# A hybrid convolution and mLSTM block: gate loads by another queue, end loads within the output projection, turns one step later, left sums in the plain stage

## The chip, the cores and the metric

The kernel runs on one core of a Trainium2 chip. The metric is device time in microseconds (us) of one execution. The engines are TensorE (PE, matrix multiplication; PEld is its weight load), VectorE (DVE), ScalarE (ACT), GpSimd (POOL) and SyncE (SP, which here only issues DMAs). Each engine works through its own queue in order. GpSimd and ACT can issue DMAs too.

## The reference

All tensors are float32; 512 tokens of 1024 features, one layer.

```python
hn = rmsnorm(x, g_mix)
proj = hn @ w_in                     # 14344 columns
(xa, ba, ca, za, q, k, v, o, zb, ig, fg, ga, gb) = split(proj)
ya = (ba * causal_short_conv(ca * xa) * silu(za)) @ w_a_out
hb = rmsnorm(mlstm_chunkwise(q, k, v, ig, fg))          # 4 heads
yb = (sigmoid(o) * hb * silu(zb)) @ w_b_out             # 2048 -> 1024
merged = sigmoid(ga) * ya + sigmoid(gb) * yb
x = x + merged @ w_o
gate = sigmoid(rmsnorm(x, g_ple) @ w_ple_gate)
x = x + gate * (p @ w_ple)
return rmsnorm(x, g_final)
```

## The kernel before

**Stages.** The work runs in one order on PE: the start and the projections of the mLSTM (0 to 100 us), its heads (to 455), the projection of ga (to 480), four convolution stages (to 642), the plain stage `w_a_out` (to 690), the heads' output `w_b_out` (to 772), the output projection `w_o` (to 815), the gate of the embedding (to 858), and the end.

**Matmuls.** Each float32 product is made of three (`mm3`, L205 to L207): both operands are cut into a high and a low part. The high part of the weights is made by ACT (`whi`, L152), the low part by DVE (`wlo`, L153), from a raw piece `wraw` that SP loads (L135) into one of four buffers. Most big products are Strassen's: seven products in place of eight, of which some need a sum of two weight pieces. The second piece is then added by an accumulating DMA that GpSimd issues (L159), or by DVE (L157). `out` makes a combined output `c` (L325) on DVE from a snapshot that ACT takes of a PSUM bank (L321: `s`, `v`).

**Order.** The engines' order is the order in which the program is written. PE works in blocks (in `w_b_out` and `w_o`, twelve matmuls of 512 columns), and after each block `step()` calls `tick()`: it starts the tasks that the block before it set off, then cuts one half of a weight piece, then takes one `yield` further each generator in `active`. So one more `yield` puts what follows one block later on every engine.

**Convolution** (`sink_conv`). `third` keeps a product `cg` in a temporary with the tag `v`, the tag of the snapshots of L321; `fourth` keeps `cx` with the tag `e`. L382 (`put`) reads `cg` last. `m`, the merged tensor of four 128x1024 rows of tokens, is in place by then and is first written in the plain stage.

**Gates.** `sink_gate(g)` writes the sigmoids of ga and gb to DRAM (`sg_d`, L716), issued by GpSimd: `sink_gate(0)` for gb early, `sink_gate(2)` for ga right before the convolution. The plain stage loads those of ga (`sga`, L985, SP) and writes m (L988). In `w_b_out`, `sink_heads` multiplies a gate of gb with the output (L1023) and adds it to m (L1024). Its gates `sgb` have two buffers, and SP loads each (L1005) after the one before it in the same buffer is used.

**Turn.** Once two rows of m are complete, `turn_half` transposes them on PE (`pth`, L1014) and cuts the result into `mg`, the left operand of `w_o`.

**Left sums.** Strassen's left operands of `w_b_out` come from `yf`, four 128x2048 tiles, and `hsf` (shown as `yhs`). `left_first` makes the first three and four differences in the plain stage, `left_heads` the others in `w_b_out` (`left_high` on ACT, `low` on DVE at L951), and four sums on DVE (L976, L980).

**Loads for the end.** Right after `w_b_out`'s code GpSimd's queue has x (`xr`, four rows of 512 KB, L1057), `gfin` (L1059) and the embedding `ple` (2 MB in one, L1061).

Of the kernel before, what the change touches and what calls it, by code (L numbers as in the profile page):

```python
# [36 lines left out]
def hybrid_block(ctx, tc, x, p, g_mix, w_in, conv_w, conv_b, w_a_out, b_gates, g_head,  # L37
# [17 lines left out]
    def close(*cs):  # L55
        for c in cs:
            c.__exit__(None, None, None)
# [200 lines left out]
    def temp(tag, name=None, dt=F32):  # L258

        return tp.tile([P, S], dt, name=name or tag, tag=tag, bufs={"c": 3}.get(tag, 2))  # L260
# [19 lines left out]
    def block_tm(lhs, post):  # L280

        pss = [None] * NT
        for c, (parts, k0) in enumerate(lhs):
            w = next_operand()
            for t in range(NT):
                if c == 0:
                    pss[t] = bank(t)
                for kt in range(HC):
                    mm3(pss[t], [u[:, k0 + kt, t * P:(t + 1) * P] for u in parts], [u[kt] for u in w],
                        c == 0 and kt == 0, c == len(lhs) - 1 and kt == HC - 1)  # L290
                step(post(t, pss[t]) if c == len(lhs) - 1 else None)
# [68 lines left out]
        product(6, acc, None, lambda i: sink(0, 2 + i, acc[i]))  # L360
        order.reverse()

    def sink_conv(c, u, v, ya):


        w = [[cw[:, j * KT + c + f:j * KT + c + f + 1] for j in range(3)] for f in range(2)]
        b = [cb[:, c + f:c + f + 1] for f in range(2)]
        part = [slice(f * H2, (f + 1) * H2) for f in range(2)]
        held = {}

        def taps(f):
            to = v[:, part[f]]
            dve.tensor_scalar(to, u[:, f, 2:], w[f][2], None, ALU.mult)
            for j in range(2):
                dve.scalar_tensor_tensor(to, u[:, f, j:j + H2], w[f][j], to, ALU.mult, ALU.add)

        def put(src, h):
            to = [t[:, c:c + 2, h * H2:(h + 1) * H2] for t in ya]
            src = src.rearrange("p (f s) -> p f s", f=2)
            act.activation(to[0], src, AF.Copy)  # L380
            yield
            dve.tensor_tensor(to[1], src, to[0].bitcast(F32), ALU.subtract)  # L382

        def split(t):
            return t.rearrange("p (f s) -> p f s", f=2)

        def first(i, src):
            if i == 0:
                held["x"] = src
                return  # L390
            dve.memset(u[:, :, :2], 0.0)
            dve.tensor_tensor(u[:, :, 2:], split(held["x"]), split(src), ALU.mult)
            for f in range(2):
                yield
                taps(f)

        def second(i, src):
            if i == 0:
                for f in range(2):
                    dve.scalar_tensor_tensor(v[:, part[f]], v[:, part[f]], b[f], src[:, part[f]], ALU.add, ALU.mult)  # L400
                return
            z = temp("e", "cz")
            act.activation(z, src, AF.Sigmoid)
            dve.tensor_tensor(v, v, src, ALU.mult)
            yield
            dve.tensor_tensor(v, v, z, ALU.mult)
            yield
            yield from put(v, 0)

        def third(i, src):  # L410
            if i == 0:
                held["b"] = src
                return
            z = temp("e", "cz")
            act.activation(z, src, AF.Sigmoid)
            g = held["g"] = temp("v", "cg")
            dve.tensor_tensor(g, held["b"], src, ALU.mult)
            yield
            dve.tensor_tensor(g, g, z, ALU.mult)

        def fourth(i, src):
            if i == 0:
                held["x"] = temp("e", "cx")
                act.activation(held["x"], src, AF.Copy)
                yield
                return
            dve.tensor_copy(u[:, :, :2], u[:, :, H2:])
            dve.tensor_tensor(u[:, :, 2:], split(held["x"]), split(src), ALU.mult)
            g = held["g"]
            for f in range(2):  # L430
                yield
                taps(f)
            yield
            for f in range(2):
                dve.scalar_tensor_tensor(g[:, part[f]], v[:, part[f]], b[f], g[:, part[f]], ALU.add, ALU.mult)
            yield
            yield from put(g, 1)

        def sink(n, t, src):
            yield from ((first, fourth), (second, third))[n][t // 2](t % 2, src)  # L440
        return sink
# [270 lines left out]
    def sink_gate(g):  # L712
        def sink(n, t, src):
            sg = temp("e", "sg") if n == 0 and t > 1 else src
            act.activation(sg, src, AF.Sigmoid)
            nc.gpsimd.dma_start(sg_d[g + n][:, t, :], sg)  # L716
            yield
        return sink

# [207 lines left out]
    cv_ctx, cvp = open_pool("conv")  # L927
    cu = cvp.tile([P, 2, H2 + 2], F32, name="cu")
    cv = cvp.tile([P, S], F32, name="cv")
    for c in range(0, KT, 2):  # L930
        strassen(hn_lhs, sink_conv(c, cu, cv, ya), True)
    close(hs_ctx, hn_ctx)


# [7 lines left out]
    def left_high(k):  # L942

        j, g = divmod(k, 2)
        a11, a21, a12, a22 = (yf[2 * g + r][:, v] for r, v in ((0, 0), (0, 1), (1, 0), (1, 1)))
        src = (a11, a12, hsf[g], a12, hsf[g], a21, a22)[j]
        both = wbp.tile([P, 2, HC, H2], F32R, name=f"l{k}", tag=f"ring{k % 3}", align_bytes=256)
        units[k] = [both[:, u] for u in range(2)]
        scale = -1.0 if j == 4 else 1.0
        act.activation(units[k][0], src, AF.Copy, scale=scale)  # L950
        return lambda: dve.scalar_tensor_tensor(both[:, 1], src, scale, both[:, 0].bitcast(F32), ALU.mult, ALU.subtract)  # L951

    def left_first():
        for _ in range(5):
            yield
        for k in range(3):
            low = left_high(k)
            yield
            low()
            yield  # L960
        for g in range(2):
            (a11, a21), a22 = (yf[2 * g][:, v] for v in range(2)), yf[2 * g + 1][:, 1]
            dve.tensor_tensor(hsf[g], a22, a21, ALU.subtract)
            yield
            dve.tensor_tensor(a21, a11, a21, ALU.subtract)
            yield

    def left_heads():
        yield
        yield  # L970
        for k in range(3, 14):
            low = left_high(k)
            yield
            low()
            if k in (4, 5):
                dve.tensor_tensor(hsf[k - 4], hsf[k - 4], yf[2 * (k - 4)][:, 0], ALU.add)  # L976
            yield
            if k in (4, 5):
                a12 = yf[2 * (k - 4) + 1][:, 0]
                dve.tensor_tensor(a12, hsf[k - 4], a12, ALU.subtract)  # L980

    def gate_conv(n):
        sga = [temp(u, "sga") for u in "sscc"]
# [6 lines left out]
        return post  # L990

    active.append(left_first())
    for n in range(2):
        block_tm([(ya, 0), (ya, HC)], gate_conv(n))


    mg = [hp.tile([P, KT, S], F32R, name=f"mg{i}", tag=t, align_bytes=256) for i, t in enumerate(("qk", "vv"))]
    sgb = deque()
    todo = deque((n, t) for n, ts in ((0, (0, 1)), (1, range(NT)), (0, (2, 3))) for t in ts)

    def load_gate():
        if todo:
            n, t = todo.popleft()
            sgb.append(temp("e", "sgb"))
            nc.sync.dma_start(sgb[-1], sg_d[n][:, t, :])  # L1005

    def turn_half(dst, src, n, h):

        ss = slice(h * H2, (h + 1) * H2)
# [10 lines left out]
    def sink_heads(n, t, src):  # L1020
        sg = sgb.popleft()
        mc = m[:, t, n * CW:(n + 1) * CW]
        dve.tensor_tensor(sg, sg, src, ALU.mult)  # L1023
        dve.tensor_tensor(mc, mc, sg, ALU.add)  # L1024
        load_gate()
        yield
        if t % 2:
            yield from turn_half(mg, m, n, t // 2)

    for _ in range(2):  # L1030
        load_gate()
    active.append(left_heads())
    strassen(units, sink_heads, groups=2)
    close(wb_ctx, cv_ctx)

    def turn_to(dst, src, n, scale):

# [15 lines left out]
    h2_ctx, h2p = open_pool("h2", side="right")  # L1053
    h2 = [h2p.tile([P, KT, S], F32R, name=f"h2_{i}", align_bytes=256) for i in range(2)]
    xr = ep.tile([P, NT, D], F32, name="xr")
    for t in range(NT):
        nc.gpsimd.dma_start(xr[:, t, :], x[0, t * P:(t + 1) * P, :])  # L1057
    gfin = ep.tile([P, D], F32, name="gfin")
    nc.gpsimd.dma_start(gfin, g_final.partition_broadcast(P))  # L1059
    ple = ep.tile([P, NT, D], F32, name="ple")  # L1060
    nc.gpsimd.dma_start(ple, ple_d)  # L1061
    ess = ep.tile([P, NT, 2], F32, name="ess")
    etot = ep.tile([P, NT], F32, name="etot")
    er = ep.tile([P, NT], F32, name="er")
    etmp = [ep.tile([P, NT], F32, name=f"etmp{i}") for i in range(3)]
    half = [slice(0, CW), slice(CW, D)]

    def add_residual(n):
        def post(t, ps):
# [6 lines left out]

    post = add_residual(0)
    pss = [None] * NT  # L1080
    w = {}
# [147 lines left out]
```

## Time and profile before

| what | value |
|---|---|
| runs | 882.72, 883.28, 887.46 us; median 883.28 |
| profiled execution | 882.37 us, span 880.6 us |
| mean granted clock of PE | 0.993 of full speed |
| PE, DVE, ACT, POOL busy | 97%, 68%, 53%, 29% of the span |
| bytes moved by DMA | 169.65 MB, 193 GB/s on the mean |

A busy share is a mean over all stages; where PE has no work is found by its waits. In a row of a timeline stand start and duration, engine, line and operation, what is written and read, the shapes, and in brackets the idle time ahead of it with what ended it. In an answer of the chain stand start, duration and the step.

### The profile page before, as it was taken

The page shows a single profiled execution, that of the slowest core. Times are in us where ns is not written, and L with a number is a line of the kernel's source. Part 1 is how long each engine was busy: PE and PEld are TensorE (multiplying, and loading weights), DVE is VectorE, ACT ScalarE, POOL GpSimd, SP SyncE. Part 2 cuts the span into 40 slices and gives each one's busy share as a digit, 9 for nine tenths or more (in the row PEclk, how much of TensorE's full clock was granted, in tenths as well). Part 3 has the DMA queues.
Part 4 walks back from the last instruction along what each step waited for, and adds up shares of the span by engine and source line. Part 5 has one row for each costly group of instructions (what it writes and reads, how often), then busy time and mean ns, then how long its engine had stood idle before and what let it go on. Part 6 is the DMA issues. An engine that isn't in the chain of part 4 may idle for free.

```text
span 880.6 us, 11798 instructions
## 1 busy us (share of the span) xinstructions
PE 853.2 (97%) x4507; PEld 731.8 (83%) x4507; DVE 600.2 (68%) x774; ACT 467.9 (53%) x674; POOL 253.2 (29%) x239
## 2 busy tenths in 40 slices
PE   7999999999999999999999999999999999879995
PEld 6877888888888888888888999999988878668885
DVE  5769586765673757836875678888876597744465
ACT  6475774646636565556665464545542555514342
POOL 4641423232322314223333424334201124100031
PEclk9999999999999999999999999999999999989998
DMA  9798987968747778787879989898995689962002
GB/s 294 257 223 222 288 207 155 217 211 189 201 144 176 150 176 188 226 192 169 205 176 249 223 176 175 200 173 183 208 379 158 124 207 197 369 224 96 1 1 96
DMA packets 100232, 169.65 MB, mean 193 GB/s; under 512 B 6160, under 2 KB 44112, under 8 KB 98768
## 3 DMA queue, kind: packets, MB, share of 16 engines
q0 software_dynamic: 38816, 76.03, 44.5%
q1 hardware_dynamic: 61360, 92.87, 31.8%
q8 instruction: 35, 0.57, 0.3%
q14 instruction: 21, 0.17, 0.1%
HBM read 153.16 MB, written 15.73 MB: 192 GB/s over the span
## 4 chain that ended last, share of the span: by engine, by line
PE 76%; DVE 9%; DMA 6%; issue 5%; ACT 3%; POOL 1%; POOLq 0%; SPq 0%; DVEq 0%; ACTq 0%
PE mm L207 23%; PE mm L206 23%; PE mm L205 23%; DVE wlo L153 4%; DMA wraw<-in_w_b_out 2%; ACT whi L152 2%; DMA wraw<-in_w_in 2%; DMA sgb<-sg_d 1%; PE pv L205 1%; PE pv L206 1%; PE pv L207 1%; PE pty L744 1%; POOL wraw L159 1%; DVE l L951 1%; PE sc L207 1%
## 5 line engine op out<-in xcount | busy, mean ns | idle before, releaser
L153 DVE TENSOR_TENSOR wlo<-wraw,whi 128x1024 fp32r<-128x1024 f32 x234 | 299.1, 1282 | 133.3 <-ACT whi L152 133.1
L152 ACT ACTIVATE whi<-wraw 128x1024 fp32r<-128x1024 f32 x236 | 246.3, 1053 | 94.9 <-PE mm L207 38.0
L159 POOL DMA_DIRECT2D wraw<-in_w_in x110 | 137.2, 1405 | 276.3 <-DVE wlo L153 207.6
L205 PE MATMUL mm<-hn_hi,whi 128*128 128x256 f32 (+1 forms) x320 | 105.1, 328 | 0.0
L207 PE MATMUL mm<-hn_hi,wlo 128*128 128x256 f32 (+1 forms) x320 | 104.4, 326 | 0.2 <-POOL wlo L153 0.2
L206 PE MATMUL mm<-hn_lo,whi 128*128 128x256 f32 (+1 forms) x320 | 104.2, 326 | 0.0
L206 PE MATMUL mm<-wlo,hs 128*128 128x512 f32 x256 | 100.1, 391 | 1.1 <-DVE wlo L153 1.0
L205 PE MATMUL mm<-whi,hs 128*128 128x512 f32 x256 | 100.2, 391 | 0.3 <-DVE c L325 0.3
L207 PE MATMUL mm<-whi,hs 128*128 128x512 f32 x256 | 99.7, 389 | 0.0
L321 ACT ACTIVATE s<-mm 128x512 f32<-128x512 f32 x78 | 46.5, 596 | 97.1 <-PE mm L207 97.0
L205 PE MATMUL mm<-whi,hn_hi 128*128 128x512 f32 x192 | 75.0, 391 | 0.0
L207 PE MATMUL mm<-whi,hn_lo 128*128 128x512 f32 x192 | 74.8, 389 | 0.0
L206 PE MATMUL mm<-wlo,hn_hi 128*128 128x512 f32 x192 | 74.8, 389 | 0.0
L207 PE MATMUL mm<-hs,wlo 128*128 128x256 f32 x256 | 72.8, 285 | 1.9 <-DVE wlo L153 1.9
L205 PE MATMUL mm<-hs,whi 128*128 128x256 f32 x256 | 72.5, 283 | 0.0
L206 PE MATMUL mm<-hs,whi 128*128 128x256 f32 x256 | 72.4, 283 | 0.0
L207 PEld LDWEIGHTS mm<-hn_hi,wlo 128*128 128x128 f32 x320 | 60.9, 190 | 5.8 <-POOL wlo L153 0.8
L206 PEld LDWEIGHTS mm<-hn_lo,whi 128*128 128x128 f32 x320 | 60.9, 190 | 4.7
L205 PEld LDWEIGHTS mm<-hn_hi,whi 128*128 128x128 f32 x320 | 60.9, 190 | 4.6
L206 PEld LDWEIGHTS mm<-wlo,hs 128*128 128x128 f32 x256 | 48.1, 188 | 11.7 <-DVE wlo L153 2.4
L205 PEld LDWEIGHTS mm<-whi,hs 128*128 128x128 f32 x256 | 48.1, 188 | 10.7 <-DVE c L325 0.7
L207 PEld LDWEIGHTS mm<-whi,hs 128*128 128x128 f32 x256 | 48.1, 188 | 10.0
(271 smaller groups left out, 1685.6 us busy)
## 6 DMA issues: line engine op xcount, KB each, us to landing
wraw<-in_w_in SPq DMA_DIRECT2D x32, 1024.0 KB, 6.0
wraw<-in_w_in POOLq DMA_DIRECT2D x62, 512.0 KB, 7.3
wraw<-in_w_in SPq DMA_DIRECT2D x48, 512.0 KB, 4.7
wraw<-in_w_in POOLq DMA_DIRECT2D x48, 256.0 KB, 5.6
wraw<-in_w_b_out SPq DMA_DIRECT2D x8, 1024.0 KB, 4.9
wraw<-in_w_b_out POOLq DMA_DIRECT2D x16, 512.0 KB, 7.8
yt_d<-yc POOLq DMA_DIRECT2D x4, 1024.0 KB, 7.6
wraw<-in_w_a_out SPq DMA_DIRECT2D x4, 1024.0 KB, 9.8
```

The costliest lines, as they stand in the source:

```text
L152: act.activation(hi, t, AF.Copy)
L153: (e_lo or dve).tensor_tensor(lo, t, hi.bitcast(F32), ALU.subtract)
L159: nc.gpsimd.dma_start(raws[to][:, ks, cs], src[:, ks, :], accum_op=ALU.add)
L205: pe.matmul(ps, lhsT=a[0], rhs=b[0], start=first, stop=False, **kw)
L206: pe.matmul(ps, lhsT=a[0], rhs=b[1], start=False, stop=False, **kw)
L207: pe.matmul(ps, lhsT=a[1], rhs=b[0], start=False, stop=last, **kw)
L321: act.activation(to[i], src, AF.Copy, scale=scale)
L744: pe.transpose(pts[v][:, t * P:(t + 1) * P], y[:, t, v * P:(v + 1) * P], ident)
L951: return lambda: dve.scalar_tensor_tensor(both[:, 1], src, scale, both[:, 0].bitcast(F32), ALU.mult, ALU.subtract)
```

## The change

In the convolution `cg` and `cx` live in parts of m. The ga gates are written to DRAM from ACT's queue. Gates of gb have four buffers, two of them new (`sgx`, in the space of the convolution's tiles) and two with the tag `e`; GpSimd loads the first four within the plain stage, and each later one into the tile that was just used. Three of the four left sums are made in the plain stage (`left_first`), into `yf` itself, and the left operands of `left_heads` come a tick later. A turn comes one step later. x is loaded in eight halves of 256 KB, ple in four rows of 512 KB, gfin last, by a generator that runs within `w_o`.

```diff
-    def sink_conv(c, u, v, ya):
+    def sink_conv(c, u, v, ya, ct):
...
-            g = held["g"] = temp("v", "cg")
+            g = held["g"] = ct[0]
...
-                held["x"] = temp("e", "cx")
+                held["x"] = ct[1]
...
-            nc.gpsimd.dma_start(sg_d[g + n][:, t, :], sg)
+            (nc.scalar if g else nc.gpsimd).dma_start(sg_d[g + n][:, t, :], sg)
...
+    ct = [m[:, 2 + i, CW:] for i in range(2)]
     for c in range(0, KT, 2):
-        strassen(hn_lhs, sink_conv(c, cu, cv, ya), True)
+        strassen(hn_lhs, sink_conv(c, cu, cv, ya, ct), True)
...
-        src = (a11, a12, hsf[g], a12, hsf[g], a21, a22)[j]
+        src = (a11, a12, hsf[g], a12, a11, a21, a22)[j]
...
         for g in range(2):
-            (a11, a21), a22 = (yf[2 * g][:, v] for v in range(2)), yf[2 * g + 1][:, 1]
+            (a11, a21), (a12, a22) = ([yf[2 * g + r][:, v] for v in range(2)] for r in range(2))
             dve.tensor_tensor(hsf[g], a22, a21, ALU.subtract)
             yield
             dve.tensor_tensor(a21, a11, a21, ALU.subtract)
             yield
+            dve.tensor_tensor(a11, hsf[g], a11, ALU.add)
+            yield
+            if g == 0:
+                dve.tensor_tensor(a12, a11, a12, ALU.subtract)
+                yield
 
     def left_heads():
         yield
-        yield
         for k in range(3, 14):
+            yield
             low = left_high(k)
             yield
             low()
-            if k in (4, 5):
-                dve.tensor_tensor(hsf[k - 4], hsf[k - 4], yf[2 * (k - 4)][:, 0], ALU.add)
-            yield
-            if k in (4, 5):
-                a12 = yf[2 * (k - 4) + 1][:, 0]
-                dve.tensor_tensor(a12, hsf[k - 4], a12, ALU.subtract)
+            if k == 3:
+                yield
+                dve.tensor_tensor(yf[3][:, 0], yf[2][:, 0], yf[3][:, 0], ALU.subtract)
...
+    def load_gate(to):
+        if todo:
+            n, t = todo.popleft()
+            nc.gpsimd.dma_start(to, sg_d[n][:, t, :])
+            sgb.append(to)
...
-    for n in range(2):
-        block_tm([(ya, 0), (ya, HC)], gate_conv(n))
+    block_tm([(ya, 0), (ya, HC)], gate_conv(0))
+    close(cv_ctx)
+    sg_ctx, sgp = open_pool("gates")
+    for i in range(4):
+        load_gate(temp("e", "sgb") if i > 1 else sgp.tile([P, S], F32, name=f"sgx{i}"))
+    block_tm([(ya, 0), (ya, HC)], gate_conv(1))
...
-    def load_gate():
-        if todo:
-            n, t = todo.popleft()
-            sgb.append(temp("e", "sgb"))
-            nc.sync.dma_start(sgb[-1], sg_d[n][:, t, :])
...
-        load_gate()
+        load_gate(sg)
         yield
         if t % 2:
+            yield
             yield from turn_half(mg, m, n, t // 2)
 
-    for _ in range(2):
-        load_gate()
...
-    for t in range(NT):
-        nc.gpsimd.dma_start(xr[:, t, :], x[0, t * P:(t + 1) * P, :])
...
-    nc.gpsimd.dma_start(gfin, g_final.partition_broadcast(P))
...
-    nc.gpsimd.dma_start(ple, ple_d)
...
+    def load_end():
+        for n in range(2):
+            for t in range(NT):
+                nc.gpsimd.dma_start(xr[:, t, half[n]], x[0, t * P:(t + 1) * P, half[n]])
+                if t % 2:
+                    yield
+        for t in range(NT):
+            yield
+            nc.gpsimd.dma_start(ple[:, t, :], ple_d[:, t, :])
+        nc.gpsimd.dma_start(gfin, g_final.partition_broadcast(P))
...
+    ends = load_end()
+    next(ends)
+    active.append(ends)
```

GpSimd's queue at the end of ga's projection, where the accumulating weight loads of the convolution (L159) follow (rows of before with -):

```order
-L716 DMA sg_d_100<-c 128x512
 L747 DMA yt_d_96<-yc 128x2048
-L716 DMA sg_d_100<-c 128x512
 L159 DMA wraw_3306<-in_w_in 128x2x512 x2
-L716 DMA sg_d_101<-c 128x512 x2
-L159 DMA wraw_3719<-in_w_in 128x2x256 x2
-L716 DMA sg_d_101<-c 128x512
-L716 DMA sg_d_100<-sg 128x512
```

The writes between the weight loads are gone from this queue; on ACT's each now stands behind its own activation.

GpSimd's queue through `w_b_out` and `w_o`, first before:

```order
L159 DMA wraw_6521<-in_w_b_out 128x2x512 x2
L159 DMA wraw_5948<-in_w_b_out 128x2x512
L159 DMA wraw_6566<-in_w_b_out 128x2x512
L159 DMA wraw_5948<-in_w_b_out 128x2x512
L159 DMA wraw_6566<-in_w_b_out 128x2x512
L159 DMA wraw_6016<-in_w_b_out 128x2x512 x2
L1057 DMA xr<-in_x 128x1024 x4
L1059 DMA gfin<-in_g_final 128x1024
L1061 DMA ple<-ple_d 128x4096
```

and after:

```order
L992 DMA sgx_6118<-sg_d_99 128x512
L159 DMA wraw_6507<-in_w_b_out 128x2x512 x2
L159 DMA wraw_5941<-in_w_b_out 128x2x512
L159 DMA wraw_6562<-in_w_b_out 128x2x512
L159 DMA wraw_5941<-in_w_b_out 128x2x512
L159 DMA wraw_6562<-in_w_b_out 128x2x512
L159 DMA wraw_6008<-in_w_b_out 128x2x512 x2
L992 DMA sgb<-sg_d_98 128x512 x2
L1074 DMA xr<-in_x 128x512 x8
L1079 DMA ple<-ple_d 128x1024 x4
L1080 DMA gfin<-in_g_final 128x1024
```

The last two gates now stand on this queue between the weights and x, and gfin stands behind ple.

DVE's queue in `w_b_out`, around the first outputs c, first before:

```order
L951 SCALAR_TENSOR_TENSOR l_6361<-yhs_5968,l_6361 128x1024
L976 TENSOR_TENSOR yhs_5968<-yhs_5968,yf_5960 128x1024
L153 TENSOR_TENSOR wlo_6397<-wraw_5948,whi_6396 128x1024
L980 TENSOR_TENSOR yf_5961<-yhs_5968,yf_5961 128x1024
L325 TENSOR_TENSOR c<-s,mm 128x512
L153 TENSOR_TENSOR wlo_6419<-wraw_5948,whi_6418 128x1024
L951 SCALAR_TENSOR_TENSOR l_6402<-yhs_5969,l_6402 128x1024
L976 TENSOR_TENSOR yhs_5969<-yhs_5969,yf_5962 128x1024
L325 TENSOR_TENSOR c<-s,mm 128x512
L153 TENSOR_TENSOR wlo_6441<-wraw_6016,whi_6440 128x1024
L980 TENSOR_TENSOR yf_5963<-yhs_5969,yf_5963 128x1024
```

and after:

```order
L983 TENSOR_TENSOR yf_5955<-yf_5954,yf_5955 128x1024
L153 TENSOR_TENSOR wlo_6379<-wraw_6168,whi_6378 128x1024
L153 TENSOR_TENSOR wlo_6399<-wraw_5941,whi_6398 128x1024
L952 SCALAR_TENSOR_TENSOR l_6384<-yhs_5960,l_6384 128x1024
L325 TENSOR_TENSOR c<-s,mm 128x512
L153 TENSOR_TENSOR wlo_6419<-wraw_5941,whi_6418 128x1024
L325 TENSOR_TENSOR c<-s,mm 128x512
L153 TENSOR_TENSOR wlo_6441<-wraw_6008,whi_6440 128x1024
```

The sums ahead of and between the outputs c are gone; one sum (L983) stands earlier.

More of the change, by code (lines that the diff above doesn't have):

```diff
@@ L974, in left_heads @@
             low()
-            if k in (4, 5):
-                dve.tensor_tensor(hsf[k - 4], hsf[k - 4], yf[2 * (k - 4)][:, 0], ALU.add)
-            yield
-            if k in (4, 5):
-                a12 = yf[2 * (k - 4) + 1][:, 0]
-                dve.tensor_tensor(a12, hsf[k - 4], a12, ALU.subtract)
+            if k == 3:
+                yield
+                dve.tensor_tensor(yf[3][:, 0], yf[2][:, 0], yf[3][:, 0], ALU.subtract)
+    sgb = deque()
+    todo = deque((n, t) for n, ts in ((0, (0, 1)), (1, range(NT)), (0, (2, 3))) for t in ts)
+    def load_gate(to):
[3 more added lines that the diff above has]
+            sgb.append(to)
     def gate_conv(n):
@@ L992, in hybrid_block @@
     active.append(left_first())
-    for n in range(2):
-        block_tm([(ya, 0), (ya, HC)], gate_conv(n))
-    mg = [hp.tile([P, KT, S], F32R, name=f"mg{i}", tag=t, align_bytes=256) for i, t in enumerate(("qk", "vv"))]
-    sgb = deque()
-    todo = deque((n, t) for n, ts in ((0, (0, 1)), (1, range(NT)), (0, (2, 3))) for t in ts)
-    def load_gate():
-        if todo:
-            n, t = todo.popleft()
-            sgb.append(temp("e", "sgb"))
-            nc.sync.dma_start(sgb[-1], sg_d[n][:, t, :])
+    block_tm([(ya, 0), (ya, HC)], gate_conv(0))
[4 more added lines that the diff above has]
+    block_tm([(ya, 0), (ya, HC)], gate_conv(1))
+    mg = [hp.tile([P, KT, S], F32R, name=f"mg{i}", tag=t, align_bytes=256) for i, t in enumerate(("qk", "vv"))]
     def turn_half(dst, src, n, h):
@@ L1024, in sink_heads @@
         dve.tensor_tensor(mc, mc, sg, ALU.add)
-        load_gate()
+        load_gate(sg)
         yield
         if t % 2:
+            yield
             yield from turn_half(mg, m, n, t // 2)
-    for _ in range(2):
-        load_gate()
     active.append(left_heads())
     strassen(units, sink_heads, groups=2)
-    close(wb_ctx, cv_ctx)
+    close(wb_ctx, sg_ctx)
     def turn_to(dst, src, n, scale):
```

## The prediction

> **What bounds the kernel now.** I read the page's first part and its chain first, to see which engine carries the span; then the list of waits of PE from 440 us on, since the change touches only that part; then the timelines of PE, DVE, ACT, POOL and SP around each of those waits; and last the transfers and the windows around the longest one.
>
> ```profile
> PE 853.2 (97%) x4507; PEld 731.8 (83%) x4507; DVE 600.2 (68%) x774; ACT 467.9 (53%) x674; POOL 253.2 (29%) x239
> PE 76%; DVE 9%; DMA 6%; issue 5%; ACT 3%; POOL 1%; POOLq 0%; SPq 0%; DVEq 0%; ACTq 0%
> ```
>
> PE is busy for 97% of the span and is 76% of the chain, and the change takes no matmul away. So the most it can win is the holes in PE's stream. The waits of PE between 440 and 880 us (engine, line, what it waited for: us in total, times, longest) are these:
>
> ```profile
> PE mm L206 <- DVE wlo L153: 6.1, 2, 5.3
> PE pth L1014 <- DVE m L1024: 3.4, 3, 1.5
> PE mm L207 <- DVE wlo L153: 1.9, 4, 0.8
> PE mm L205 <- DVE c L325: 0.6, 1, 0.6
> ```
>
> Together 12.0 us in ten holes. A hole costs a little more than its idle time, because the pipeline of matmuls fills again. The first hole of the turn measures that (start, duration, in brackets the idle time and its releaser):
>
> ```profile
> 717.84 0.27 PE L1014 MATMUL pth<-ident,m 128*128 128x128 f32 x1
> 719.04 0.99 PE L1014 MATMUL pth<-ident,m 128*128 128x128 f32 x7 [0.93 <-DVE m L1024]
> ...
> 718.30 0.69 DVE L1024 TENSOR_TENSOR m<-m,sgb 128x512 f32<-128x512 f32 x1
> ```
>
> Seven transposes in 0.99 us are about 0.12 us each ((0.99 - 0.27)/6). From start to start 1.20 us pass, so the hole costs 1.20 - 0.12 = 1.08, which is its idle 0.93 and 0.15 of refilling. I add 0.15 to each hole. DVE's row says why it is there: the sum into m ends at 718.99, and the turn that reads m was already next on PE.
>
> **The change part by part.** The turn comes one step later, so a block of twelve matmuls stands between the sum and its transposes. How long is a block?
>
> ```profile
> 735.00:750.00 15.00, 15.00 (x68) 12.43 (x67) 9.66 (x10) 6.89 (x8) 5.17 (x5) 1.00 1.12 209
> 660.00:695.00 35.00, 35.00 (x156) 28.97 (x155) 20.42 (x21) 9.47 (x10) 4.87 (x4) 1.00 0.57 139
> ```
>
> The columns of a window are its length, busy time and count of PE, PEld, DVE, ACT and POOL, then granted clock, DMA share and GB/s. In the first 68 matmuls take 15.00 us, 0.22 each, so a block is 2.65 us, more than the 1.5 us of the longest wait on m. All three waits go: 3.4 + 3 x 0.15 = -3.8. The DVE cuts of the turn follow a step later too; their result is first read in the output projection, some blocks on, so I cost that at nothing (bounds: nothing, and one pair of DVE operations as the sum above, 1.4 us, if the last turn were late).
>
> The left sums are the 0.6 hole:
>
> ```profile
> 709.97 1.23 DVE L976 TENSOR_TENSOR yhs<-yhs,yf 128x1024 f32<-128x1024 f32 x1
> 711.11 0.68 DVE L325 TENSOR_TENSOR c<-s,mm 128x512 f32<-128x512 f32 x1
> ...
> 711.85 0.50 PE L205 MATMUL mm<-whi,l 128*128 128x512 f32 x1 [0.59 <-DVE c L325]
> ```
>
> PE waits for c, which frees a PSUM bank, and c stands behind a sum of 1.23 us. The sum goes, so 0.59 + 0.15 = -0.75. Three of four sums go to the plain stage: 3 x 1.23 = 3.7 us of DVE. The second window above covers it, with DVE busy for 20.4 of 35.0 us and no hole of PE in it; the fourth stays in an early tick of w_b. Without that cover the worst is the 3.7. Left units that are prepared a tick later still come a block ahead of their use: nothing.
>
> In the convolution four products wait for a snapshot:
>
> ```profile
> ACT v L321 <- DVE cu L391: 9.3, 3, 3.1
> ...
> 538.62 0.69 DVE L382 TENSOR_TENSOR ya<-cg,ya 128x512 fp32r<-128x512 f32 x1
> ...
> 539.42 0.60 ACT L321 ACTIVATE v<-mm 128x512 f32<-128x512 f32 x1 [3.11 <-DVE cu L391]
> ...
> 544.72 0.39 PE L207 MATMUL mm<-hs,wlo 128*128 128x256 f32 x1 [0.40 <-DVE wlo L153]
> ```
>
> The snapshot v needs the buffer that cg held, and L382 reads cg until 539.31. ACT then stands 3.11 us with the weight split behind it, and PE misses its weights 5 us on, by 0.40. With cg and cx in m nothing has to be freed. Three times 0.40 + 0.15 makes -1.65. Bounds: nothing, if the split is late for its own sake, and 1.65. I take all of it, since the idle 3.11 is eight times the hole.
>
> The eight gate writes move from GpSimd's queue to ACT's:
>
> ```profile
> 479.28 1.59 POOL L716 DMA_DIRECT2D sg_d<-c  x1
> 480.45 3.50 POOL L159 DMA_DIRECT2D wraw<-in_w_in  x2
> ...
> 478.83 0.60 ACT L715 ACTIVATE sg<-mm 128x512 f32<-128x512 f32 x1 [0.65 <-PE mm L207]
> 489.85 2.01 ACT L152 ACTIVATE whi<-wraw 128x1024 fp32r<-128x1024 f32 x2 [3.65 <-DMA wraw<-in_w_in]
> ...
> 492.22 0.39 PE L207 MATMUL mm<-hs,wlo 128*128 128x256 f32 x1 [0.76 <-DVE wlo L153]
> ...
> L985 SPq DMA_DIRECT2D sga<-sg_d x8: 319/546/3259, 637.9 to 663.0; - x8
> ```
>
> The accumulating weight loads at 480.45 stand behind the writes on POOL, land 9 us later, and the hole at 492.22 (0.76 + 0.15 = 0.9) is theirs. What an issue costs ACT is not in the trace; the nearest are SP's issues of tiles of this size, 0.32 to 3.26 us, median 0.55 (last row). ACT sits idle 0.65 ahead of a gate's activation, which hides the median. So the price lies between -0.9 and 8 x (3.26 - 0.65) = +21. I take -0.7, as the median is what most issues cost. The DMA page of the Trainium skill (DMA: Bandwidth & Descriptors, Issuing engines are not separate DMA queues) says that another issuing engine saves only the time of the sequencer, since the same engines carry the bytes; by it this term would be nearer nothing, and the sum 0.7 higher. No run here shows it yet.
>
> The weights at 752 us are the one hole that I expect to stay:
>
> ```profile
> 734.02 6.15 POOL L159 DMA_DIRECT2D wraw<-in_w_b_out  x5 [1.98 <-issue]
> ...
> 735.48 14.49 DMA wraw<-in_w_b_out
> ...
> 750.05 2.01 ACT L152 ACTIVATE whi<-wraw 128x1024 fp32r<-128x1024 f32 x2 [2.96 <-DMA wraw<-in_w_b_out]
> ...
> 752.43 0.50 PE L206 MATMUL mm<-wlo,l 128*128 128x512 f32 x1 [0.76 <-DVE wlo L153]
> ```
>
> Five accumulating loads leave in a row and one lands after 14.49 us. PE arrives earlier by what it wins ahead of it in this stage (1.08 of the turn and the 0.75), the loads partly follow, since the buffers come free as PE goes on. If they did not follow at all the hole would grow by 1.8, if wholly by nothing. A second thing takes part: two gate loads now stand between these accumulations on POOL, and those that SP issued are gone. I take +0.5, range -0.9 (the hole goes) to +1.8.
>
> The largest is the gate that comes late:
>
> ```profile
> 754.08 2.19 POOL L1057 DMA_DIRECT2D xr<-in_x  x4 [13.91 <-issue]
> 763.14 0.34 SPq L1005 DMA_DIRECT2D sgb<-sg_d  x1
> 776.44 0.69 DVE L1023 TENSOR_TENSOR sgb<-sgb,mm 128x512 f32<-128x512 f32 x1 [6.94 <-DMA sgb<-sg_d]
> ...
> 773.35 0.39 PE L205 MATMUL mm<-whi,mg 128*128 128x512 f32 x1
> 779.04 0.79 PE L206 MATMUL mm<-wlo,mg 128*128 128x512 f32 x1 [5.31 <-DVE wlo L153]
> 783.47 0.49 PE L207 MATMUL mm<-whi,mg 128*128 128x512 f32 x1
> ...
> 780.00:782.00 2.00, 2.00 (x6) 1.55 (x5) 1.97 (x4) 0.00 (x0) 0.00 (x0) 0.50 0.82 252
> ...
> xr<-in_x POOLq DMA_DIRECT2D x4, 512.0 KB, 8.4
> ple<-ple_d POOLq DMA_DIRECT2D x1, 2048.0 KB, 15.9
> sgb<-sg_d SPq DMA_DIRECT2D x3, 256.0 KB, 12.1
> ```
>
> x and ple (last rows: KB each, median us to landing, 754 to 780 us) leave from 754 on. The gate issued at 763.14 lands 13.2 us later, DVE stands 6.94 us for it with a weight split behind it, and PE loses 5.69 - 0.22 = 5.5. Then the granted clock is 0.50: from 779.04 to 783.47 PE works 4.43 us at half speed, which costs another 2.2. After the change four gates are in place before w_b; the next two leave at its ninth and tenth block, and the last two once DVE has used the tiles again, about 750, ahead of x. The first of these was due at 776.44 - 6.94 = 769.5, and PE gets there 6.4 us earlier by the other terms: 763. So 12 us are left for it to land, and x leaves after both: -7.7. x itself is released by a sum on DVE at about 763, in halves; its four loads took 8.4 us, and the residual reads it first about 775. So 3 us to spare, and ple and gfin are read some 40 us later. Bound: if x were late by the 8.4 again, +5.
>
> Sum: -3.8 - 0.75 - 1.65 - 0.7 + 0.5 - 7.7 = -14.1. The profiled execution took 882.37 us, so 868.3. The median of the runs is 883.28, 0.9 above it; I put half of that on top and forecast **868.5**. What a measurement can tell from no change is 0.5%, 4.4 us: under 878.9 is faster, over 887.7 slower.
>
> **The rivals.** *New waits in w_b, 871 to 874.* The hole at 752 grows by the whole 1.8, and DVE, relieved of the 6.94, finds cuts, m sums and splits on top of each other at the start of w_o: one more hole of a few DVE operations (0.69 and 1.23 us each), 1 to 3 us. For it: DVE is busy 9.66 of 15 us in the window from 735. Against it: PE has no hole between 719 and 751 in spite of that.
>
> *The gates still come late, 874 to 876.* The last two gates now stand on POOL behind the accumulations of the row at 734.02, and if they land after the same 14.49 us, at 764 to 765, DVE waits again and most of the 7.7 returns. For it: the DMA share of 1.12 from 735 to 750. Against it: after 750 nothing else large is in flight before x. A page of the Trainium skill (SBUF — State Buffer, SBUF: two separate sides) says that a transfer issued from GpSimd can be starved of descriptors while DVE runs a copy in its two-port mode, and advises SP or ACT; starved gates would bring back the same wait, and the same 874 to 876. The rows bear that out little: POOL's x took 8.4 us for 512 KB, SP's gates 12.1 for 256 KB.
>
> *It changes nothing, 880 to 884.* The same bytes have to move between 740 and 810 us; if they only meet the weights of w_o in place of the gates, the large hole moves, and the small ones stay because DVE is late for its own sake.
>
> *Slower, 888 or more: ACT is held by its own issues.* ACT's queue is in order, and splits stand behind the writes. Eight writes have to eat 14.1 + 4.4 = 18.5 us, that is 2.3 each beyond the idle 0.65, so 3.0 us per issue; SP's longest is 3.26. At that it would be 889. Against it is the median 0.55.
>
> **How the numbers follow.** The forecast 0.62 (its own range 865.5 to 870.5: the low end if the hole at 752 goes and each term is full, the high end with the bounds of GA and x partly used), new waits 0.20, late gates 0.08, nothing 0.05, ACT held 0.05. The range 865.5 to 874.5 holds the first two. Faster 0.90, same 0.05, slower 0.05.
>
> **What would show it.** The turn's transposes find m ready; PE's waits on c and at 544, 585 and 626 us are gone; ACT's wait ahead of v is gone; DVE has no wait on a gate's DMA; the granted clock stays at 1.00 after w_b; the hole at the second accumulation of w_b is 1 to 2 us. The prediction is wrong if ACT shows idle time behind its DMA issues between 462 and 482 us, if DVE waits on sgb or xr, or if PE shows a new hole in the first blocks of w_o.

## The result and the profile after

| | before | after |
|---|---|---|
| runs, us | 882.72 to 887.46, median 884.61 (4) | 868.64 to 872.46, median 871.07 (4) |
| ratio | 1 | 0.9841, 95% interval 0.9803 to 0.9880 |
| profiled execution's span | 880.6 | 869.7 |

The kernel is 1.6% faster, 13.5 us by the medians. 868.5 was forecast: the median after, 871.07, lies in the stated range of 865.5 to 874.5, but 0.6 above the forecast's own narrower one (865.5 to 870.5). The waits of PE from 440 us on, in the profile after (engine, line, what it waited for: us in total, times, longest):

```profile
PE mm L206 <- DVE wlo L153: 0.8, 1, 0.8
PE mm L207 <- DVE wlo L153: 0.8, 1, 0.8
PE mm L205 <- ACT whi L152: 0.2, 1, 0.2
```

Of 12.0 us are left 1.8. No wait on m, on c or on a late gate is left, and none in the convolution behind its start. The three that remain are these, from PE's timeline:

```profile
494.94 0.28 PE L206 MATMUL mm<-hs,whi 128*128 128x256 f32 x1
495.98 0.39 PE L207 MATMUL mm<-hs,wlo 128*128 128x256 f32 x1 [0.76 <-DVE wlo L153]
...
750.83 0.49 PE L205 MATMUL mm<-whi,l 128*128 128x512 f32 x1 [0.15 <-ACT whi L152]
752.09 0.50 PE L206 MATMUL mm<-wlo,l 128*128 128x512 f32 x1 [0.77 <-DVE wlo L153]
```

The first is the hole at the start of the convolution, as long as before (0.76). The other two are the weights of w_b that were expected to stay. The windows of the plain stage and around the old late gate show the clock and DVE:

```profile
660.00:695.00 35.00, 35.00 (x157) 28.96 (x155) 25.26 (x26) 9.32 (x9) 4.83 (x4) 1.00 0.58 159
774.00:798.00 24.00, 24.00 (x116) 20.06 (x115) 8.85 (x10) 8.30 (x15) 0.53 (x1) 1.00 0.64 249
```

DVE took the moved sums in the plain stage (25.3 us busy in 35, before 20.4), with PE busy throughout. PE has no hole in w_o, and the clock stays at 1.00 there. GpSimd and DVE there:

```profile
749.49 0.60 POOL L992 DMA_DIRECT2D sgb<-sg_d  x1 [10.32 <-DVE m L1032]
753.66 0.57 POOL L992 DMA_DIRECT2D sgb<-sg_d  x1 [3.58 <-DVE m L1032]
765.78 4.24 POOL L1074 DMA_DIRECT2D xr<-in_x  x8 [11.55 <-issue]
```

```profile
764.55 0.69 DVE L1032 TENSOR_TENSOR m<-m,sgx 128x512 f32<-128x512 f32 x1
766.29 0.68 DVE L1031 TENSOR_TENSOR sgb<-sgb,mm 128x512 f32<-128x512 f32 x1
```

The last two gates leave at 749 and 754, as forecast, and are used from 766 on with no wait; x leaves at 765.8, half a microsecond after the end of DVE's sum of the second `sgx` tile.

**How executions are compared below.** Everything up to the first gate of ga is the same code in both kernels, yet its sigmoid (ACT, L715) starts at 451.4 us in the profile before and at 455.3 in the one after. Over the fourteen profiles of this study it lies between 451.4 and 455.3. So I take it as a landmark and give "from the landmark", the rest of the span: 429.2 before, 414.4 after, 14.7 less. The losses of PE are start-to-start times over the usual spacing (0.227 us for 512 columns, 0.120 for 256, 0.11 for a transpose):

| loss of PE, us | start of conv. | in conv. | c | turns | near 750 | w_o | from the landmark |
|---|---|---|---|---|---|---|---|
| before | 0.9 | 1.7 | 1.0 | 3.9 | 1.0 | 7.6 | 429.2 |
| after | 0.9 | 0 | 0 | 0 | 1.3 | 0 | 414.4 |

The columns make 13.9 of the 14.7. Most of the rest is the matmul behind each hole, which starts about 0.1 us late as well and is not in them.

### The profile page after: what moved, and what is told of

It reads as the page before. It is cut to its first block, busy times and chain, and to the rows that moved or that the text cites. A ratio compares the mean times of both kernels' runs of the same rounds, so it can differ in the third digit from the quotient of the medians.

```text
span 869.7 us, 11799 instructions
## 1 busy us (share of the span) xinstructions
PE 852.3 (98%) x4507; PEld 732.3 (84%) x4507; DVE 599.8 (69%) x774; ACT 468.4 (54%) x674; POOL 255.8 (29%) x246
## 4 chain that ended last, share of the span: by engine, by line
PE 80%; DMA 6%; issue 4%; DVE 4%; ACT 2%; POOL 2%; POOLq 0%; SPq 0%; DVEq 0%; ACTq 0%
PE mm L206 24%; PE mm L207 24%; PE mm L205 24%; DMA wraw<-in_w_in 3%; DMA wraw<-in_w_b_out 2%; DVE wlo L153 2%; PE pv L205 1%; ACT whi L152 1%; PE pv L206 1%; PE pv L207 1%; POOL wraw L159 1%; PE pty L744 1%; DMA sg_d<-c 1%; DMA pin<-in_p 0%; PE sc L207 0%
## 5 line engine op out<-in xcount | busy, mean ns | idle before, releaser
L159 POOL DMA_DIRECT2D wraw<-in_w_in x110 | 136.0, 1402 | 289.1 <-DVE wlo L153 218.5
```

The source lines that it names most:

```text
L159: nc.gpsimd.dma_start(raws[to][:, ks, cs], src[:, ks, :], accum_op=ALU.add)
```

## The experiments

Twelve runs follow, one of them the changed kernel again. The ratios to the kernel before are within one chip each.

### 1 to 5: what made the gate late

*Gates by SP again, two buffers* (the changed kernel with this part undone):

```diff
-    for i in range(4):
-        load_gate(temp("e", "sgb") if i > 1 else sgp.tile(...))
...
-            nc.gpsimd.dma_start(to, sg_d[n][:, t, :])
+            to = temp("e", "sgb")
+            nc.sync.dma_start(to, sg_d[n][:, t, :])
```

> The changed kernel with the gates of gb as they were: two buffers, loaded by SP, each released by the use two gates before; x, ple and gfin stay within the output projection. Theory A (the hole of 5.5 us came from x, ple and gfin standing ahead of the gate in the transfers): a gate lands in about 6 us, the last two leave at about 762 and 764, DVE waits 0 to 2 us, PE loses at most 1.5 us and the clock stays at 1.00: 871 to 873 us. Rival B (the late release of two buffers makes it): DVE waits 5 us or more, PE loses 5 and the clock falls: 876 to 879 us.

878.58 us, ratio to before 0.9927 (0.9900 to 0.9954). That is what the rival said, but the timeline of GpSimd and the ones of SP and DVE show that the test was not the one that I meant:

```profile
755.08 4.35 POOL L1073 DMA_DIRECT2D xr<-in_x  x8 [17.70 <-ACT l L951]
...
763.25 0.34 SPq L994 DMA_DIRECT2D sgb<-sg_d  x1
...
765.72 0.34 SPq L994 DMA_DIRECT2D sgb<-sg_d  x1
...
770.75 0.69 DVE L1028 TENSOR_TENSOR sgb<-sgb,mm 128x512 f32<-128x512 f32 x1 [3.92 <-DMA sgb<-sg_d]
...
779.30 0.69 DVE L1028 TENSOR_TENSOR sgb<-sgb,mm 128x512 f32<-128x512 f32 x1 [6.00 <-DMA sgb<-sg_d]
```

x left at 755, with all its code within w_o: GpSimd had nothing ahead of it, and its memory was released by the left operands (ACT l) and not, as after the change, by a gate's sum. So the bytes stood ahead of the gates as ever.

*x, gfin and ple as before, at once after w_b's code; gates as changed*:

```diff
+    for t in range(NT):
+        nc.gpsimd.dma_start(xr[:, t, :], x[0, t * P:(t + 1) * P, :])
+    nc.gpsimd.dma_start(gfin, ...)
+    nc.gpsimd.dma_start(ple, ple_d)
...
-    ends = load_end()
```

> The changed kernel with x, gfin and ple loaded as before, all at once right behind the last matmuls of w_b on GpSimd's queue; the gates stay on GpSimd's queue with four buffers. Theory A (what stood ahead of the gate was the trouble, and the gates are now gone before): no wait of DVE on a gate, the weights of w_o are loaded long before; 870 to 872 us as the changed kernel. Rival B (these 4.5 MB need the place within w_o): weights of w_o or of the gate of the embedding come late, a hole of 2 us or more: 873 us or more.

870.36 us, ratio 0.9832 (0.9805 to 0.9859), from the landmark 414.9. No wait of DVE on a gate.

```profile
764.41 2.10 POOL L1064 DMA_DIRECT2D xr<-in_x  x4 [11.54 <-issue]
766.51 0.53 POOL L1066 DMA_DIRECT2D gfin<-in_g_final  x1
767.03 0.53 POOL L1068 DMA_DIRECT2D ple<-ple_d  x1
```

x leaves at 764.4 here too. The changed kernel took 870.98 on the same chip (below), so the generator in w_o, the halves, the rows of ple and the place of gfin do nothing to the time once the gates are loaded as changed.

*Both undone*:

> Both undone: gates by SP with two buffers, and x, gfin and ple at once before w_o. Both theories: DVE's wait of 5 to 7 us on a gate is back, PE loses about 5.5 us and runs at half clock after it: 7 to 8 us over the changed kernel, 877 to 880 us. If it is less than 3 us over, the gate's hole was not made by these two parts alone.

879.65 us, ratio 0.9938 (0.9914 to 0.9963). In PE's list this row holds the gate's hole and one of 0.8 near 750:

```profile
PE mm L206 <- DVE wlo L153: 8.7, 2, 7.9
```

One wait of 7.9 us, 8.7 us over the changed kernel on the same chip. The first of these three kernels alone costs 7.6, and the second nothing, so nearly all of it comes with the gates.

*The changed kernel once more*:

> The changed kernel itself once more, on the same chip as the three others. In the two profiles so far the gates of ga begin 3.8 us later after the change, though nothing ahead of them was changed. If that is a spread between executions, the landmark will lie elsewhere here, and spans between landmark and end will agree within 0.5 us with the first profile of the changed kernel; if the change causes it, the landmark is 3 to 4 us behind that of before again. Time 868 to 873 us.

870.98 us, ratio 0.9833 (0.9806 to 0.9859). The landmark is at 452.9 in place of 455.3, so the late start of the first profile is a spread between executions. From the landmark 415.9 pass, though, 1.4 more and not within 0.5: the loss near 750 is 3.6 in place of 1.3, and the one at the start of the convolution 0.2 in place of 0.9. The two rows near 750 (compare 0.15 and 0.77 in the first profile):

```profile
748.28 0.50 PE L205 MATMUL mm<-whi,l 128*128 128x512 f32 x1 [0.92 <-ACT whi L152]
749.54 0.50 PE L206 MATMUL mm<-wlo,l 128*128 128x512 f32 x1 [0.76 <-DVE wlo L153]
```

How the two losses hang together is taken up with the last three experiments.

*Gates by SP with two buffers, and x held*. A GpSimd operation of one column that reads m after the sum of the sixth gate stands ahead of x:

```diff
+    held_x = ep.tile([P, 1], F32, name="held_x")
+    pool.tensor_tensor(held_x, m[:, 3, CW:CW + 1], mhalf[:, :1], ALU.mult)
     ends = load_end()
```

> In the run with the gates on SP, x and ple still left at 755 to 764 us, ahead of the last two gates: place in the code does not hold a queue that has nothing else to do. Here one small GpSimd operation on m stands ahead of x, so that x leaves at about 765 as in the changed kernel; gates by SP with two buffers, as before the change. Theory A (the bytes ahead of the gates make their lateness): the last but one gate leaves at 763 and lands in 6 to 7 us, DVE waits about 3 us once and 1 to 2 us for the last; PE loses 1 to 3 us in w_o: 872 to 874 us. Rival B (two buffers are too few, whatever is in flight): DVE waits 10 us in sum as in the run before, 878 us.

870.47 us, ratio 0.9820 (0.9791 to 0.9850): all of the gate's gain is back, with the queue and the buffers of before. The timelines of GpSimd and SP, and DVE's use:

```profile
767.99 4.39 POOL L1073 DMA_DIRECT2D xr<-in_x  x8
...
764.42 0.34 SPq L994 DMA_DIRECT2D sgb<-sg_d  x1
...
766.89 0.34 SPq L994 DMA_DIRECT2D sgb<-sg_d  x1
...
772.85 0.69 DVE L1028 TENSOR_TENSOR sgb<-sgb,mm 128x512 f32<-128x512 f32 x1 [2.39 <-DMA sgb<-sg_d]
```

The last but one gate, issued at 764.4, is used at 767.9 without a wait; the last costs DVE 2.4 us and PE 0.3. So theory A holds, and two buffers are enough once x is held. (Its span from the landmark is 418.8, since the losses at the start of the convolution, 1.7, and near 750, 4.6, are longer than in the others; neither lies in what was edited.)

### 6 to 8: the turn and the sums

*No added step ahead of the turn*:

```diff
         if t % 2:
-            yield
             yield from turn_half(mg, m, n, t // 2)
```

> The changed kernel without the added step ahead of a turn. If the turn's term holds, three waits of PE on m are back, about 0.93 us idle and 1.08 lost each (the third no longer has a gate's wait in it): 3.2 us over the changed kernel, 874 us. If the block in between only moved the loss elsewhere (cuts that come later, splits behind them), it is within 1 us of the changed kernel, 871.

869.56 us, ratio 0.9818 (0.9795 to 0.9840), from the landmark 414.5: no longer than the changed kernel. PE's list has no wait on m, and the first turn shows why (DVE, then PE):

```profile
713.54 0.69 DVE L1032 TENSOR_TENSOR m<-m,sgx 128x512 f32<-128x512 f32 x1
...
715.44 0.82 PE L1022 MATMUL pth<-ident,m 128*128 128x128 f32 x6
```

The sum ends at 714.2, and the transposes come at 715.4: DVE is 1.2 us early, where it was 1.15 late before the change. The step that was to remove 3.8 us removes nothing measurable in this kernel.

*Left sums and left operands as before, turn a step later*:

```diff
-            dve.tensor_tensor(a11, hsf[g], a11, ALU.add)
...
+            if k in (4, 5):
+                dve.tensor_tensor(hsf[k - 4], hsf[k - 4], yf[2 * (k - 4)][:, 0], ALU.add)
```

> The changed kernel with the left sums and the left operands as before the change (four sums of 1.23 us on DVE in w_b, the low halves a tick earlier); the turn stays a step later. Only PE's wait on c is back (0.6 us idle, 0.75 lost, and 0.3 a little later); the turn finds m ready thanks to its step: 1 us over the changed kernel. If the sums also hold the turn, a wait on m is back as well.

869.59 us, ratio 0.9828 (0.9796 to 0.9860), from the landmark 416.2, 1.8 over the first profile of the changed kernel and 0.4 over the second. The wait on c is back as expected (0.75 and 0.30 lost), none on m:

```profile
PE mm L205 <- DVE c L325: 0.6, 1, 0.6
```

*Both undone*:

> Sums and left operands as before, and the turn without its added step. The run without the step alone showed no wait on m. Theory E (the turn waited since DVE was late with the sums and with a low half ahead of the gate; either remedy is enough): with both undone two waits on m are back, 0.93 idle and 1.08 lost each, and the wait on c, in all 3.2 us over the changed kernel, 873 to 875 us. Rival F (the turn waited for the gates' late landing alone): no wait on m, 1 us over.

871.33 us, ratio 0.9853 (0.9826 to 0.9880), from the landmark 415.8. PE's list:

```profile
PE pth L1019 <- DVE m L1029: 1.7, 2, 0.9
PE mm L205 <- DVE c L325: 0.6, 1, 0.6
PE mm L207 <- DVE wlo L153: 0.3, 1, 0.3
```

Two waits on m are back (1.09 and 0.93 lost), as theory E said: either remedy is enough. The time is not 3.2 us longer, though: the loss near 750 is gone. PE loses 2.1 on c and the first turn ahead of the weights near 750, and these, at which it lost 1.3 and 3.6 in the two profiles of the changed kernel, are there when it comes. The second turn, 0.9, lies behind them.

### 9: the convolution alone

The kernel before with only this:

```diff
-            g = held["g"] = temp("v", "cg")
+            g = held["g"] = ct[0]
...
-                held["x"] = temp("e", "cx")
+                held["x"] = ct[1]
```

> The kernel before with cg and cx in m, and nothing else. If the term holds, PE's three waits of 0.40 us on wlo in the convolution and ACT's three waits ahead of v are gone, 1.7 us under the kernel before (2 us shorter from the first ga gate to the plain stage's first sga multiplication); if the split is late for its own sake the three waits stay. The later holes stay as before the change. The hole at the start of the convolution (0.93 in the profile before) shows by how much it differs between executions of the same code.

882.66 us, ratio 0.9971 (0.9947 to 0.9995), by the ratio 2.6 us less (0.4 to 4.7). PE has no wait between 500 and 640 us where it had three of 0.40, and ACT's snapshots now wait for PE alone:

```profile
ACT v L321 <- PE mm L207: 14.3, 8, 4.2
```

All of the 1.7 came from the buffer. The stretch from the landmark to the first multiplication with sga, announced 2 us shorter, is 3.1 longer (205.5 to 208.6). At the start of the convolution this execution lost 3.5 us with the code of before, against 0.9 in the first profile, and half speed followed:

```profile
496.00:502.00 6.00, 5.24 (x25) 5.04 (x25) 3.80 (x4) 1.82 (x3) 2.42 (x2) 0.51 1.03 164
```

Matmul by matmul from the landmark, this execution falls 5.1 us behind the one before there, 2.5 by the longer hole and 2.6 by the half speed. At the three places it then gains 1.9, the 1.7 and the late matmul behind each hole. That leaves 3.2, against the 3.1. So the hole at the start of the convolution is not a fixed quantity.

### 10 to 12: the two holes that are left

*Gate write from another tile*. In the changed kernel DVE waits for a gate's way to DRAM, since `c` is held by it (ACT's queue, then DVE):

```profile
473.88 0.33 ACTq L716 DMA_DIRECT2D sg_d<-c  x1
...
480.06 0.69 DVE L325 TENSOR_TENSOR c<-s,v 128x512 f32<-128x512 f32 x1 [2.75 <-DMA sg_d<-c]
```

```diff
-            sg = temp("e", "sg") if n == 0 and t > 1 else src
+            sg = temp("e", "sg") if n == 0 and t > 1 or g and (n, t) == (1, 0) else src
```

> The changed kernel; the third of ACT's gate writes to DRAM leaves from a tile with the tag e in place of c. DVE's wait of 2.3 to 3.0 us for that write (c's buffer) is then gone. If that wait made the hole at 492 to 496 us (0.2 to 0.9 lost in the runs so far), the accumulating loads leave 2 to 3 us earlier and the hole is gone: 0.2 to 0.9 us. If those loads land late because the transfers are full there, it stays between 0.2 and 0.9.

869.14 us, ratio 0.9827 (0.9798 to 0.9856). DVE's wait is gone, the accumulating loads leave at 479.3 in place of 482.2, which is 1.9 us earlier from the landmark (GpSimd, first the changed kernel, then this one), and the hole at 492 to 496 us is 0:

```profile
482.18 4.90 POOL L159 DMA_DIRECT2D wraw<-in_w_in  x4 [15.75 <-DVE wlo L153]
```

```profile
479.26 2.43 POOL L159 DMA_DIRECT2D wraw<-in_w_in  x2 [13.90 <-DVE wlo L153]
```

So it was that write. But the loss near 750 is 2.2 here, and from the landmark 414.1 pass.

*b12 before b11 in w_b*:

```diff
-    adds = {..., 8: [(b11, b21, 0), (b12, b22, 1)], 9: [(b11, b21, 1)]}
+    adds = {..., 8: [(b12, b22, 1)], 9: [(b11, b21, 0), (b11, b21, 1)]}
```

> The changed kernel with one change of its own: of the accumulating loads in w_b, the two halves of b12 are issued before the ones of b11 that are needed later. Theory C (the hole at 750 us comes from where in GpSimd's row of five that load stands): the load leaves 1.2 us earlier with fewer bytes ahead, the hole of 1.3 to 3.7 us shrinks under 0.5: 868 to 870 us. Rival D (all accumulating loads share the bandwidth and end together at about 748): the hole stays at 1 to 2 us, 871 us.

868.89 us, ratio 0.9817 (0.9790 to 0.9844), from the landmark 414.6. PE's timeline:

```profile
754.66 0.50 PE L206 MATMUL mm<-wlo,l 128*128 128x512 f32 x1 [0.27 <-DVE wlo L153]
...
761.84 0.50 PE L206 MATMUL mm<-wlo,l 128*128 128x512 f32 x1 [1.44 <-DVE wlo L153]
```

The old hole is gone, as theory C said: counted in matmuls of w_b, the pair that waited (270 and 271) loses nothing. Two new holes open behind it, of 0.4 and 1.6 us, 24 and 48 matmuls later; the loads that the edit puts back are the likely reason, which no run shows. So rival D fails, but the order of the row decides which piece is late, and something still is.

*All three* (no added step of the turn either):

> The changed kernel with the third gate write from e, the order of b12 and b11 turned, and no added step of the turn. The holes near 492 and 750 shrink as far as the runs apart showed (sum of 3 us to 2), nothing else changes: 867 to 870 us, 0 to 2 us under the changed kernel, which a measurement cannot tell from none.

867.63 us, ratio 0.9811 (0.9787 to 0.9834), its interval overlapping that of the changed kernel; from the landmark 412.6, the shortest of all, with one hole of 0.7 left:

```profile
759.64 0.50 PE L206 MATMUL mm<-wlo,l 128*128 128x512 f32 x1 [0.55 <-DVE wlo L153]
```

Whether it is faster than the changed kernel these runs do not settle; it is faster than before.

## Why the prediction was right, step by step

**The sum.** -14.1 was forecast; from the landmark the change took 14.7 and 13.3 us in two profiles, and the medians fell by 13.5. The forecast of 868.5 is 2.6 under the median after. 2.0 of that is the base: the sum was made against the execution of 882.37 and the median of three runs, while the four in the comparison have 884.61, and eleven or thirteen on other chips 884.52 and 886.36. Its profile had the earliest landmark of all. That the sum comes so close is in part luck: the gate writes brought nothing of their 0.7, and what made up for it, a second wait of 0.3 after the one on c and the late matmul behind each hole, was in no term.

**The rivals.** The measured median lies at the edge of the band of "new waits in w_b" (871 to 874), but not for its reason: no hole opens in w_o, which its time needed. The growth of the hole near 750, its other half, was 0.3 in the first profile and 2.6 in the second, against its 1.8. DVE waits for no gate, and ACT's issues stay far under the 3.0 us of the slower rival, so these two did not come.

**The gate (-7.7): size right, cause only half.** The hole and the half clock went as sized (7.6); undoing gates and end loads together cost 8.7. The named cause, the bytes ahead of the gate, is shown by the run with x held. What was wrong is the credit that the two parts of the change got: neither the generator within w_o nor GpSimd's queue with four buffers is needed as such. What the new tiles do is hold x back: x's memory lies where the second of them was, and so x can't leave before that gate is used. This I read from the times. In all nine profiles with these tiles x leaves 1.23 to 1.24 us after the start of DVE's last sum from such a tile, be that at 761.5 or at 765.8, and long after the last gate load ahead of it on the queue (748 to 754); with the tiles gone it leaves at 754 to 755. No run moved x's memory alone.

**The turn (-3.8): the holes went, the step that was named did not do it.** This is the step that failed, "a block of twelve matmuls stands between the sum and its transposes". The block is there, but without it there is no wait either. DVE was late at the first turn since two sums and a low half stood ahead of the gates' products, at the second with a low half there, and at the third since a gate was late (DVE, before):

```profile
712.84 1.22 DVE L980 TENSOR_TENSOR yf<-yhs,yf 128x1024 f32<-128x1024 f32 x1
...
716.44 1.22 DVE L951 SCALAR_TENSOR_TENSOR l<-yf,l 128x1024 fp32r<-128x1024 f32 x1
...
766.95 0.69 DVE L1023 TENSOR_TENSOR sgb<-sgb,c 128x512 f32<-128x512 f32 x1 [2.70 <-DMA sgb<-sg_d]
```

The other parts of the change removed those. I had charged the turn and the sums as if they were apart; they are two remedies for one lateness of DVE. So the size of this term came out without the step that it was charged to, and that is luck.

**The sums (-0.75) and the convolution (-1.65): right.** 0.75 on c, and another 0.30 on weights 5 us later that came back with it; and 1.7.

**The gate writes (-0.7): wrong, nothing.** ACT's issues took 0.33 us each and fit its idle time, so the slower rival was far off. But the hole in the profile after was 0.76 idle as before. In the kernel before, the load did stand right behind a write, as I had read. But without it, it lands no earlier, 38.2 us after the landmark against 38.3 (the chain before, then its last step after):

```profile
479.88 0.50 POOL sg_d L716
...
480.45 0.44 POOL wraw L159
...
481.20 8.55 DMA wraw<-in_w_in
```

```profile
484.37 9.13 DMA wraw<-in_w_in
```

The step that was wrong is that the writes alone held the loads. DVE's split, which releases them, waited for c, whose buffer the write held, as the run with the write from e shows for the changed kernel. That wait was there before the change too, 2.12 us from GpSimd's queue against 2.75 from ACT's (DVE, before):

```profile
475.65 0.69 DVE L325 TENSOR_TENSOR c<-s,v 128x512 f32<-128x512 f32 x1 [2.12 <-DMA sg_d<-c]
```

The Trainium skill (DMA: Bandwidth & Descriptors, Issuing engines are not separate DMA queues), by which another issuing engine saves little, came out nearer than my reading.

**The weights near 750 (+0.5): under.** +0.3 in the first profile, +2.6 in the second, +0.5 to +1.2 in four others of the changed kernel's kin (end loads early, both undone, no added step, gate write from e). Of the +2.6, which lies outside the term's range, 1.5 are half speed, for which no term stood. I assumed that the loads follow PE in part. From before to after they do: PE comes to the late pair of matmuls 4.5 and 5.4 us earlier in the two profiles, counted from the landmark, and the second of the pair starts 4.2 and 4.3 earlier. Among the ten profiles with the changed kernel's order of loads they hardly follow: the matmul ahead of the pair starts anywhere from 293.9 to 296.9 us after the landmark, and the second of the pair at 296.5 to 297.5 in eight of them (in one, sums and turn undone, without a wait). So most of what PE gains ahead of those loads it waits for at them, and removing a single hole ahead of 750 paid little. The other two, 298.7 with the sums late and 299.5 with the gates by SP and x held, stay open.

## What to carry to other kernels

Before crediting a gain to an edit, undo that edit alone: here three of the change's parts (the step ahead of the turn, the loads written within w_o, the gates' queue) were not needed for the holes that they stood beside, the last of them once x was held by other means. Nor does the place of a line hold a load back: x left at 755 us from a line that stands in w_o, with nothing ahead of it on its queue and its memory free, and at 768 behind one small operation that waited for a gate's sum. And holes on one engine are not added up past a transfer that sets its own time: here the next late arrival, at 296.5 to 297.5 us from the landmark, took most of what single edits gave ahead of it.

## What the hardware showed that I had not expected

The granted clock fell after a short loss as well. In the second profile of the changed kernel two losses within 2.3 us, 0.92 and 0.76 us of idle time, were followed by half speed, which the first profile, with 0.15 and 0.77 of idle time, does not have (windows of the second, then of the first; the clock is the 0.72 and the 1.00):

```profile
749.00:755.00 6.00, 5.46 (x17) 4.36 (x18) 5.78 (x7) 3.61 (x5) 0.57 (x1) 0.72 1.09 308
```

```profile
749.00:755.00 6.00, 5.08 (x22) 3.65 (x21) 4.34 (x6) 4.40 (x6) 1.17 (x2) 1.00 1.10 264
```

By the spacing of eight matmuls (0.43 in place of 0.23) that cost 1.5 us more than the idle time. The same happened at this place in two of the runs with the gates by SP (losses of 1.6 and 1.0 us, and of 2.2 and 1.0 with x held). It did not with 1.2 and 1.0 in the run of the gate write from e, against 1.1 and 1.0 here, nor after a single loss of 2.5 us at 771 in the run with the gates by SP, where the granted clock stays at 1.00 up to the next hole. So the sum of the losses alone does not decide it, and what does stays open.
